# A hybrid block on one core: the token sums, first weights and weight sums of the seven products placed and ordered anew

## The chip, the cores and the metric

The kernel runs on one core of a Trainium2 chip. Its time is device microseconds of one execution. Five engines each work off a queue of their own in order: TensorE (PE: matmuls; PEld are its weight loads), VectorE (DVE), ScalarE (ACT), GpSimd (POOL) and SyncE (SP, which issues most transfers). They wait for each other by semaphores.

## The reference, cut to what matters

```python
def swiglu(x, w_gate, w_up, w_down):
    return (jax.nn.silu(x @ w_gate) * (x @ w_up)) @ w_down

def reference(x, ...):
    h = x                                             # 512 tokens x 1024
    f = swiglu(rms_norm(h, ffn1_norm_pre), ffn1_w_gate, ffn1_w_up, ffn1_w_down)   # hidden size 2816
    h = h + 0.5 * rms_norm(f, ffn1_norm_post)
    m = hybrid_mixer(rms_norm(h, mix_norm_pre), ...)  # attention and convolution, not touched here
    h = h + rms_norm(m, mix_norm_post)
    f = swiglu(rms_norm(h, ffn2_norm_pre), ffn2_w_gate, ffn2_w_up, ffn2_w_down)
    return h + 0.5 * rms_norm(f, ffn2_norm_post)
```

All is float32. Every operand of a matmul is kept as a high and a low part, and a product is three matmuls (high x high, high x low, low x high; `mm3`).

## The kernel before

**Stages.** The first feed-forward block (`ffn`), the mixer, the second `ffn`. The hidden dimension has 22 tiles of 128; each needs one block of gate weights and one of up weights, 128 x 1024 float32 of 512 KB. Weight blocks come in the order of use through three buffers (`raws`) by transfers on SyncE. `split` makes the two parts: ScalarE copies the high part, VectorE subtracts it and so gives the low part. The parts live in a ring of six pairs (`ring`, `whi` and `wlo`).

**Tiles 0 to 2** (`CLASSIC` = 3) are computed directly, each from a pair of blocks with 24 matmuls a block: "pair 0", "pair 1" and "pair 2" (the third pair) below. `hidden` ends a pair: a Silu on ScalarE, a multiplication on VectorE into `hid`. The first `ffn` opens with two pairs (its list of steps has four entries), on the first half of the tokens (`lo` = 0), then on the second half (`lo` = HALF), and computes pair 2 after them on all 512 tokens at once. The second `ffn` has six entries, so all three pairs are in that part. The tokens' own transposes (`turned0`, `turned2`) are steps in between.

**Tiles 3 to 21** go through seven products in place of eight, a scheme in Strassen's manner over two halves of the tokens and two of the inner dimension. `token_sums` makes, once, four sums s1 to s4 of the quadrants of u (`join` adds high and low part back together first; `early` joins the first half of the tokens, `first` the second half and makes s1, s2; `second` makes s4 and s3; `third` splits s3 into the place of quadrant (0, 1) of u). `weight_sums` makes for each tile four half blocks of weight sums: t13 (two subtractions on VectorE) and t24 (two on GpSimd, the second from the first). Each tile then has the operands b, t13, t24 (128 x 1024) and b22 (128 x 512), each split by `high` (ScalarE) and `low` (VectorE).

**A period.** A product is twelve matmuls with 256 columns. Period j (the loop in `seven_products`) runs the first three products of tile j (`first_products`: b x a11, t13 x s1, t24 x s2), the two last of tile j-1 (`third_products`), and two more of tile j (`second_products`: t13 x s3, then b x a12). Between them VectorE reads partial results out of a bank before the next product accumulates into it: the additions `add(xs[j][:, q[1]], ...)` and the like, line 346, tile xn. In the same period the operands of tile j+1 are made. The order is that of the code (`in_order`: TensorE, VectorE and ScalarE are not rescheduled there, GpSimd nowhere).

**After the run** `row_product` multiplies by the down weights; `act` splits rows of `hid`. Its weights are fetched and split by `prefetch`. The pools `ffn_gu` (sums, t13, t24, b22) and `ffn_d` (act) share memory one after the other.

**Norm weights.** `gpool` has two buffers of 128 x 1024 (name gain). `constants`, called in the middle of the first `ffn`, loads the gains of post and mix into them, on ScalarE's queue, with the mixer's constants and the table of relative positions (rel, tile xn, two small steps on VectorE, lines 563 and 564).

Of the kernel before, what the change touches and what calls it, by code (L numbers as in the profile page):

```python
# [8 lines left out]
F32 = mybir.dt.float32  # L9
# [43 lines left out]
def kernel(  # L53
# [238 lines left out]
    def token_sums(u, hid, gu):  # L292
# [8 lines left out]
        place3 = quadrant(u, 0, 1)  # L301
# [26 lines left out]
        return parts[0], parts[1], place3, parts[2], (early, first, second, third)  # L328

    def seven_products(u, sums, hid, gu, j0):  # L330
# [4 lines left out]
        s1, s2, s3, s4, (_, _, _, late) = sums  # L335
# [9 lines left out]
        def add(out, a, b, eng=nc.vector, op=ALU.add):  # L345
            eng.tensor_tensor(out=out, in0=a, in1=b, op=op)  # L346

        def weight_sums(j):

            gate, up = raw[j]  # L350
            t13 = gu.tile([P, 1024], F32, name="t13")
            t24 = gu.tile([P, 1024], F32, name="t24")
# [5 lines left out]
            ops[j] = {"b": (pair_tiles(), gate), "t13": (pair_tiles(), t13), "t24": (pair_tiles(), t24),  # L358
                      "b22": (b22, up[:, hi])}
# [34 lines left out]
        for n in ("b", "t13", "t24", "b22"):  # L394
            if n == "b":
                load(j0)
                weight_sums(j0)
            high(j0, n)
            low(j0, n)
        load(j0 + 1)  # L400
        for j in range(j0, NF + 1):
            p, n = j - 1, j + 1
            old, now, new = p >= j0, j < NF, n < NF
            if old:
                x, (g1, g2, g3) = xs[p], g[p]
                y = ys[p] = wide()
                add(x[:, q[2]], g2[:, q[0]], x[:, q[0]])
                add(y[:, q[3]], g3[:, q[0]], x[:, q[2]])
                silu(y[:, q[0]], g1[:, q[0]])
            if now:  # L410
                first_products(j)
            if new:
                weight_sums(n)
                high(n, "b")
                low(n, "b")
# [573 lines left out]
```

## Time and profile before

| | us |
|---|---|
| times of the runs shown | 1071.84, 1072.8, 1467.72 |
| their median | 1072.8 |
| the profiled execution | 1069.87 |
| its span | 1068.1 |
| TensorE busy in it | 1037.4 |

The profile is of one execution. A row of a timeline has start and length in us, engine, line, operation, tiles (written <- read), size, and, where the engine stood idle before, for how long and whom the instruction waited for. A matmul's row is longer than its share, since matmuls overlap in the pipe: read starts, not lengths. "First head" below is the stretch from the end of the classic pairs to the first full period in the first `ffn`, "second head" that in the second; "tail" is where the products end and the down weights begin.

### The profile page before, as it was taken

What the parts mean: (1) busy time and instruction counts of PE and PEld (TensorE: products, weight loads), DVE (VectorE), ACT (ScalarE), POOL (GpSimd) and SP (SyncE); (2) the same over time, 40 slices, a digit from 0 to 9 for tenths busy, and PEclk for the clock granted to TensorE, in tenths of its full rate; (3) what the DMA queues carried; (4) which work ended last, traced back from release to release, by engine and by line L of the source; (5) the groups of instructions that cost most, each with busy time, mean ns of one, the idle gap of its engine ahead of it and who ended that gap; (6) DMA issues with size and microseconds to landing.
All of it is one profiled execution on the core that took longest, in us unless ns stands there. A gap on an engine that the chain in (4) does not pass through costs nothing.

```text
span 1068.1 us, 16197 instructions
## 1 busy us (share of the span) xinstructions
PE 1037.4 (97%) x6527; PEld 942.2 (88%) x6527; DVE 801.9 (75%) x1112; ACT 479.2 (45%) x785; POOL 163.2 (15%) x118
## 2 busy tenths in 40 slices
PE   9869999999999999999999999998999999999997
PEld 8769999998888899888888888898999999978886
DVE  7589999997333477999969777479899999773324
ACT  6244444445222343477885354344444444352211
POOL 1043343340000010000000100012242442200000
PEclk9979999999999999999999999999899999999999
DMA  6133333334433133332321135131323333343301
GB/s 236 64 99 100 99 100 119 100 100 129 127 99 99 40 118 119 100 97 88 98 87 49 52 104 177 55 119 41 99 99 104 114 99 102 98 158 99 99 20 79
DMA packets 30046, 106.42 MB, mean 100 GB/s; under 512 B 3457, under 2 KB 4105, under 8 KB 29970
## 3 DMA queue, kind: packets, MB, share of 16 engines
q1 hardware_dynamic: 27648, 100.41, 29.5%
q10 hardware_dynamic: 2322, 4.97, 1.5%
q8 instruction: 51, 0.84, 0.3%
q14 instruction: 25, 0.20, 0.1%
HBM read 103.25 MB, written 2.12 MB: 99 GB/s over the span
## 4 chain that ended last, share of the span: by engine, by line
PE 88%; DVE 4%; issue 4%; DMA 2%; ACT 1%; POOL 1%; DVEq 0%; POOLq 0%; SPq 0%
PE ps L214 26%; PE ps L132 19%; PE ps L131 18%; PE ps L133 18%; PE ps L196 3%; DMA raw<-in_w 1%; DVE wlo L367 1%; PE ps L790 1%; PE ps L773 1%; POOL t L346 1%; PE ps L176 1%; PE ps L763 0%; PE ps L762 0%; DVE ul L93 0%; DMA h<-in_x 0%
## 5 line engine op out<-in xcount | busy, mean ns | idle before, releaser
L131 PE MATMUL ps<-uh,whi 128*128 128x256 f32 (+1 forms) x960 | 300.6, 313 | 15.7 <-DVE xn L346 11.7
L133 PE MATMUL ps<-uh,wlo 128*128 128x256 f32 (+1 forms) x960 | 298.1, 310 | 4.1 <-DVE wlo L367 4.1
L132 PE MATMUL ps<-ul,whi 128*128 128x256 f32 (+1 forms) x960 | 298.2, 311 | 1.0 <-DVE ul L93 1.0
L93 DVE TENSOR_TENSOR wlo<-raw,whi 128x1024 fp32r<-128x1024 f32 x108 | 131.5, 1220 | 134.5 <-ACT whi L92 134.4
L131 PEld LDWEIGHTS ps<-uh,whi 128*128 128x128 f32 x960 | 185.8, 194 | 24.8 <-ACT whi L363 14.4
L133 PEld LDWEIGHTS ps<-uh,wlo 128*128 128x128 f32 x960 | 185.6, 193 | 13.4 <-DVE wlo L367 4.4
L132 PEld LDWEIGHTS ps<-ul,whi 128*128 128x128 f32 x960 | 185.7, 193 | 9.5 <-DVE ul L93 1.6
L214 PE MATMUL ps<-whi,act 128*128 128x512 f32 x704 | 190.3, 390 | 1.8 <-ACT act L92 1.8
L92 ACT CAST whi<-raw 128x1024 fp32r<-128x1024 f32 x108 | 112.7, 1050 | 169.3 <-PE ps L214 131.9
L346 POOL TENSOR_TENSOR t<-raw,t 128x512 f32<-128x512 f32 x76 | 142.9, 1880 | 288.4 <-DVE t L346 285.4
L214 PEld LDWEIGHTS ps<-whi,act 128*128 128x128 f32 x704 | 131.9, 188 | 29.2 <-issue 2.2
L367 DVE TENSOR_TENSOR wlo<-t,whi 128x1024 fp32r<-128x1024 f32 x76 | 132.9, 1748 | 1.5 <-ACT whi L363 1.4
L363 ACT CAST whi<-t 128x1024 fp32r<-128x1024 f32 x76 | 79.7, 1049 | 116.3 <-PE ps L132 99.7
L214 PE MATMUL ps<-wlo,act 128*128 128x512 f32 x352 | 109.6, 389 | 0.0
L346 DVE TENSOR_TENSOR xn<-ps,xn 128x256 f32<-128x256 f32 x190 | 76.6, 416 | 17.3 <-PE ps L133 16.1
L367 DVE TENSOR_TENSOR wlo<-raw,whi 128x1024 fp32r<-128x1024 f32 x38 | 86.7, 2280 | 2.8 <-ACT whi L363 2.8
L601 DVE SCALAR_TENSOR_TENSOR acc<-c,ch,acc 128x512 f32<-128x512 f32 x120 | 86.1, 746 | 1.5
L214 PEld LDWEIGHTS ps<-wlo,act 128*128 128x128 f32 x352 | 66.1, 188 | 13.8
L159 POOL TENSOR_TENSOR rstd<-ms,mhalf 128x1 f32<-128x1 f32 x24 | 15.1, 628 | 388.9 <-DVE ms L155 388.5
L392 ACT ACTIVATE xn<-ps 128x256 f32<-128x256 f32 x38 | 14.6, 385 | 94.2 <-DVE xn L346 81.1
L346 DVE TENSOR_TENSOR t<-raw 128x512 f32<-128x512 f32 x76 | 48.8, 683 | 0.7 <-DVE b22l L367 0.6
L131 PE MATMUL ps<-s1h,whi 128*128 128x256 f32 x152 | 43.5, 286 | 0.0
(185 smaller groups left out, 1700.3 us busy)
## 6 DMA issues: line engine op xcount, KB each, us to landing
raw<-in_w SPq DMA_DIRECT2D x132, 512.0 KB, 3.5
raw<-in_wm SPq DMA_DIRECT2D x52, 512.0 KB, 3.6
gain<-in_gains ACTq DMA_DIRECT2D x5, 512.0 KB, 3.8
h<-in_x SPq DMA_DIRECT2D x4, 512.0 KB, 7.0
out<-h SPq DMA_DIRECT2D x3, 512.0 KB, 2.6
bias<-tab_d ACTq DMA_DIRECT2D x8, 128.0 KB, 3.1
bias<-tab_d ACTq DMA_DIRECT2D x8, 112.0 KB, 3.1
out<-xn SPq DMA_DIRECT2D x1, 256.0 KB
```

Of the source, the lines that this page charges most:

```text
L92: nc.scalar.copy(out=hi, in_=src)
L93: nc.vector.tensor_tensor(out=lo, in0=src, in1=hi.bitcast(F32), op=ALU.subtract)
L131: nc.tensor.matmul(ps, a[0], b[0], start=start, stop=False, **kw)
L132: nc.tensor.matmul(ps, a[0], b[1], start=False, stop=False, **kw)
L133: nc.tensor.matmul(ps, a[1], b[0], start=False, stop=stop, **kw)
L159: nc.gpsimd.tensor_tensor(r, ms, mhalf, op=ALU.pow)
L196: nc.tensor.matmul(ps[:, lo:hi], w[wi][:, k * P:(k + 1) * P], u[ui][:, k, lo:hi], start=i == 0 and k == 0, stop=i == 2 and k == KD - 1)
L214: nc.tensor.matmul(acc[n], a[ai], w[bi][:, n * 512:(n + 1) * 512], start=start and i == 0, stop=stop and i == 2)
L346: eng.tensor_tensor(out=out, in0=a, in1=b, op=op)
L363: nc.scalar.copy(out=h_, in_=src)
L367: nc.vector.tensor_tensor(out=l_, in0=src, in1=h_.bitcast(F32), op=ALU.subtract)
L601: nc.vector.scalar_tensor_tensor(acc[:, j, :], cs[j][:, w:w + S], wc, acc[:, j, :], op0=ALU.mult, op1=ALU.add)
```

## The change

- The joins of the first half of the tokens (`early`) become a step ahead of the last transposed tokens' split: in place of `step()` stands `(step or early)()`, and the lists have a None there.
- `third` goes: s3 is split in `second`, into the two buffers of `gpool`, not into u. The gains are loaded after the products (`late1`, `late2`).
- `weight_sums` becomes `sums13` and `sums24`, all four subtractions on VectorE; in a period t24's sums stand between b's and t13's parts.
- The preparation of tile 3 (`before`, a generator) is pulled forward: b, t13 and the t24 sums between pair 0's and pair 1's `hidden`, t24's parts ahead of `second`, b22 after pair 2's `hidden`. In the first `ffn` that is ahead of pair 2's products.
- In the last period the first two blocks of down weights and the first two rows of `hid` (`down_parts`, into a pair of the ring) are split while the products still run.

```diff
-        place3 = quadrant(u, 0, 1)
+        third = [gpool.tile([P, 4, HALF], F32R, name="gain") for _ in range(2)]
...
             nc.vector.tensor_tensor(out=s3, in0=whole[0, 0], in1=whole[0, 1], op=ALU.subtract)
-
-        def third():
-            split(*place3, s3)
+            split(*third, s3)
...
-        def weight_sums(j):
...
-            add(t24[:, lo], up[:, hi], t13[:, lo], nc.gpsimd, ALU.subtract)
-            add(t24[:, hi], gate[:, hi], t24[:, lo], nc.gpsimd, ALU.subtract)
+        def sums13(j):
...
+        def sums24(j):
+            gate, up = raw[j]
+            t24 = gu.tile([P, 1024], F32, name="t24")
+            add(t24[:, lo], up[:, hi], ops[j]["t13"][1][:, lo], op=ALU.subtract)
+            add(t24[:, hi], gate[:, hi], t24[:, lo], op=ALU.subtract)
...
+        def before():
+
+            load(j0)
+            sums13(j0)
+            parts(j0, "b")
+            parts(j0, "t13")
+            sums24(j0)
+            yield
+            parts(j0, "t24")
+            yield
+            parts(j0, "b22")
+            load(j0 + 1)
+
+        def down_parts(n):
+
+            for pair in pair_tiles()[0:n]:
+                a = pair[:, lo], pair[:, hi]
+                split(*a, hid[:, len(acts), :])
+                acts.append(a)
+
+        def periods():
...
+                if now:
+                    first_products(j)
+                if new:
+                    sums13(n)
+                    parts(n, "b")
+                elif now:
+                    prefetch(1)
+                if now:
+                    xs[j] = wide()
+                    nc.scalar.copy(out=xs[j][:, q[0]], in_=g[j][0][:, q[0]])
+                if new:
+                    sums24(n)
+                    parts(n, "t13")
+                elif now:
                     prefetch(2)
+                if now:
+                    add(xs[j][:, q[1]], g[j][1][:, q[0]], xs[j][:, q[0]])
+                if old:
+                    third_products(p)
+                    add(x[:, q[3]], g2[:, q[0]], x[:, q[0]])
+                if new:
+                    parts(n, "t24")
+                elif now:
+                    down_parts(2)
...
                         if lo == 0:
-                            early()
                             prefetch(2 * CLASSIC - head)
                             first()
+                    hidden(0, pss[0])
+                    next(before)
+                    hidden(1, pss[1])
                 if between:
                     with tc.issue_after(later["silu"].ins):
                         between()
                 with in_order():
-                    for j in range(head // 2, CLASSIC):
-                        ps = two_banks()
-                        for i in range(2):
-                            columns(weight(0), u, ps[i])
-                        hidden(j, ps)
+                    next(before)
                     second()
-                    seven_products(u, sums, hid, gu, CLASSIC)
-
+                    for j in range(2, CLASSIC):
+                        if j >= len(pss):
+                            pss.append(two_banks())
+                            for ps in pss[j]:
+                                columns(weight(0), u, ps)
+                        hidden(j, pss[j])
+                    next(before, None)
+                    periods()
+
+            late()
...
+    def late1():
+        later["post"] = gain(1)
+        later["mix"] = gain(2)
```

How the order moves at three places (names as in the program; the numbers tell buffers apart).

VectorE in the first head, up to the addition `xn<-ps` that reads tile 3's bank ahead of its second products; before, from the sum s3 (`hid<-hid`) on:

```order
L323 TENSOR_TENSOR hid_209<-hid_209 128x1024
L346 TENSOR_TENSOR t13_568<-raw_566,raw_564 128x512
L346 TENSOR_TENSOR t13_568<-raw_566 128x512
L367 TENSOR_TENSOR wlo_577<-raw_564,whi_576 128x1024
L367 TENSOR_TENSOR wlo_579<-t13_568,whi_578 128x1024
L367 TENSOR_TENSOR wlo_581<-t24_569,whi_580 128x1024
L367 TENSOR_TENSOR b22l_575<-raw_566,b22h_574 128x512
L346 TENSOR_TENSOR t13_633<-raw_592,raw_590 128x512
L346 TENSOR_TENSOR t13_633<-raw_592 128x512
L367 TENSOR_TENSOR wlo_642<-raw_590,whi_641 128x1024
L367 TENSOR_TENSOR wlo_644<-t13_633,whi_643 128x1024
L346 TENSOR_TENSOR xn_649<-ps_595,xn_649 128x256
```

and after the change, from s3 on (`gain` is the new place of the third sum's parts):

```order
L323 TENSOR_TENSOR hid_209<-hid_209 128x1024
L93 TENSOR_TENSOR gain_220<-hid_209,gain_219 128x1024
L474 TENSOR_TENSOR hid_209<-xn_585,ps_536 128x512
L372 TENSOR_TENSOR b22l_512<-raw_495,b22h_511 128x512
L344 TENSOR_TENSOR t13_633<-raw_592,raw_590 128x512
L344 TENSOR_TENSOR t13_633<-raw_592 128x512
L372 TENSOR_TENSOR wlo_637<-raw_590,whi_636 128x1024
L344 TENSOR_TENSOR t24_644<-raw_592,t13_633 128x512
L344 TENSOR_TENSOR t24_644<-raw_590,t24_644 128x512
L372 TENSOR_TENSOR wlo_639<-t13_633,whi_638 128x1024
L344 TENSOR_TENSOR xn_642<-ps_595,xn_642 128x256
```

The third sum's low part, pair 2's multiplication (L474) and two t24 subtractions have come ahead of the addition; the splits of tile 3's b, t13 and t24 have moved further up.

VectorE in the first head at pair 1's multiplication and the table of positions (`xn<-xn`); before:

```order
L453 TENSOR_TENSOR hid_209<-xn_491,ps_222 128x512
L563 TENSOR_SCALAR xn_500<-xn_500 8x257
L564 COPY xn_500<-xn_500 8x383
L453 TENSOR_TENSOR hid_209<-xn_557,ps_508 128x512
L321 TENSOR_TENSOR hid_209<-hid_209 128x1024
L93 TENSOR_TENSOR s4l_218<-hid_209,s4h_217 128x1024
```

and after the change:

```order
L344 TENSOR_TENSOR t24_508<-raw_495,t13_497 128x512
L344 TENSOR_TENSOR t24_508<-raw_493,t24_508 128x512
L474 TENSOR_TENSOR hid_209<-xn_515,ps_224 128x512
L586 TENSOR_SCALAR xn_520<-xn_520 8x257
L587 COPY xn_520<-xn_520 8x383
L372 TENSOR_TENSOR wlo_514<-t24_508,whi_513 128x1024
L321 TENSOR_TENSOR hid_209<-hid_209 128x1024
L93 TENSOR_TENSOR s4l_218<-hid_209,s4h_217 128x1024
```

The table's two steps stood ahead of pair 2's multiplication; now t24's low part and s4 follow them.

VectorE at the tail of the first run, before (`wlo<-raw` are down weights, `xn<-ps` the additions, `act` the first row of `hid`):

```order
L346 TENSOR_TENSOR xn_2731<-ps_2677,xn_2731 128x256
L346 TENSOR_TENSOR xn_2792<-ps_2678,xn_2731 128x256
L435 TENSOR_TENSOR hid_209<-xn_2792 128x512
L93 TENSOR_TENSOR wlo_2869<-raw_2866,whi_2868 128x1024
L93 TENSOR_TENSOR wlo_2875<-raw_2872,whi_2874 128x1024
L346 TENSOR_TENSOR xn_2835<-ps_2797,xn_2835 128x256
L93 TENSOR_TENSOR wlo_2950<-raw_2947,whi_2949 128x1024
L346 TENSOR_TENSOR xn_2902<-ps_2798,xn_2835 128x256
L346 TENSOR_TENSOR xn_2835<-ps_2797,xn_2835 128x256
L93 TENSOR_TENSOR wlo_2956<-raw_2953,whi_2955 128x1024
L346 TENSOR_TENSOR xn_2902<-ps_2798,xn_2835 128x256
L93 TENSOR_TENSOR act_2959<-hid_209,act_2959 128x512
```

and after the change:

```order
L93 TENSOR_TENSOR wlo_2836<-raw_2833,whi_2835 128x1024
L93 TENSOR_TENSOR wlo_2844<-raw_2841,whi_2843 128x1024
L344 TENSOR_TENSOR xn_2839<-ps_2795,xn_2839 128x256
L344 TENSOR_TENSOR xn_2722<-ps_2675,xn_2722 128x256
L93 TENSOR_TENSOR whi_2873<-hid_209,whi_2873 128x512
L93 TENSOR_TENSOR wlo_2874<-hid_209,wlo_2874 128x512
L344 TENSOR_TENSOR xn_2790<-ps_2676,xn_2722 128x256
L456 TENSOR_TENSOR hid_209<-xn_2790 128x512
L344 TENSOR_TENSOR xn_2839<-ps_2795,xn_2839 128x256
L344 TENSOR_TENSOR xn_2906<-ps_2796,xn_2839 128x256
L344 TENSOR_TENSOR xn_2839<-ps_2795,xn_2839 128x256
L344 TENSOR_TENSOR xn_2906<-ps_2796,xn_2839 128x256
```

The down weights and the first two rows of `hid` (`whi_2873`, `wlo_2874`) are split ahead of the last tile's additions.

## Rows read from the trace of the kernel before

**Rows 1.** The page: its busy time by engine, and a DMA issue.

```profile
PE 1037.4 (97%) x6527; PEld 942.2 (88%) x6527; DVE 801.9 (75%) x1112; ACT 479.2 (45%) x785; POOL 163.2 (15%) x118
...
gain<-in_gains ACTq DMA_DIRECT2D x5, 512.0 KB, 3.8
```

**Rows 2.** TensorE's waits: us in total, times, longest.

```profile
PE ps L131 <- DVE xn L346: 11.7, 4, 5.5
PE ps L133 <- DVE wlo L367: 4.1, 1, 4.1
PE ps L131 <- ACT whi L363: 4.0, 1, 4.0
PE ps L214 <- ACT act L92: 1.8, 2, 1.0
...
PE ps L132 <- DVE ul L93: 1.0, 2, 0.5
```

**Rows 3.** Timeline of TensorE, first head.

```profile
47.53 0.39 PE L133 MATMUL ps<-uh,wlo 128*128 128x512 f32 x1
...
67.64 0.55 PE L131 MATMUL ps<-uh,whi 128*128 128x256 f32 x1 [4.18 <-DVE xn L346]
...
73.16 0.28 PE L131 MATMUL ps<-uh,whi 128*128 128x256 f32 x1
```

**Rows 4.** Timeline of TensorE, second head.

```profile
749.52 0.55 PE L131 MATMUL ps<-uh,whi 128*128 128x256 f32 x1 [5.45 <-DVE xn L346]
...
755.39 0.28 PE L131 MATMUL ps<-uh,whi 128*128 128x256 f32 x1
```

**Rows 5.** Busy time of PE, PEld, DVE, ACT, POOL, then clock, DMA.

```profile
65.60:72.40 6.80, 4.27 (x18) 4.01 (x19) 5.69 (x8) 1.56 (x2) 0.48 (x1) 0.50 0.37 105
749.50:755.00 5.50, 4.99 (x22) 4.72 (x22) 4.39 (x7) 0.06 (x1) 0.07 (x1) 0.50 0.47 153
100.00:240.00 140.00, 140.00 (x1169) 140.00 (x1168) 138.07 (x167) 63.88 (x98) 52.94 (x28) 1.00 0.34 105
```

**Rows 6.** Timeline of TensorE, tail of the first run.

```profile
255.79 0.39 PE L131 MATMUL ps<-uh,whi 128*128 128x256 f32 x1 [1.04 <-DVE xn L346]
...
259.92 0.47 PE L214 MATMUL ps<-whi,act 128*128 128x512 f32 x1 [0.95 <-ACT act L92]
```

**Rows 7.** Timeline of VectorE and GpSimd, one period inside the first run.

```profile
93.09 0.88 DVE L346 TENSOR_TENSOR xn<-ps,xn 128x256 f32<-128x256 f32 x2
93.88 1.28 DVE L346 TENSOR_TENSOR t<-raw 128x512 f32<-128x512 f32 x2
95.08 2.32 DVE L367 TENSOR_TENSOR wlo<-raw,whi 128x1024 fp32r<-128x1024 f32 x1
97.32 2.31 DVE L367 TENSOR_TENSOR wlo<-t,whi 128x1024 fp32r<-128x1024 f32 x1
...
100.29 1.23 DVE L367 TENSOR_TENSOR wlo<-t,whi 128x1024 fp32r<-128x1024 f32 x1
...
103.16 0.88 DVE L346 TENSOR_TENSOR xn<-ps,xn 128x256 f32<-128x256 f32 x2
...
94.69 3.86 POOL L346 TENSOR_TENSOR t<-raw,t 128x512 f32<-128x512 f32 x2 [6.20 <-DVE t L346]
```

**Rows 8.** Timeline of VectorE, first head.

```profile
34.58 0.68 DVE L453 TENSOR_TENSOR hid<-xn,ps 128x512 f32<-128x512 f32 x1
...
39.33 0.28 DVE L563 TENSOR_SCALAR xn<-xn 8x257 f32<-8x257 f32 x1 [1.52 <-DMA xn<-in_rel]
...
50.96 1.23 DVE L93 TENSOR_TENSOR s4l<-hid,s4h 128x1024 fp32r<-128x1024 f32 x1 [1.11 <-ACT s4h L92]
```

**Rows 9.** Timeline of VectorE and ScalarE, second head.

```profile
719.83 1.29 DVE L93 TENSOR_TENSOR ul<-ps,uh 128x512 fp32r<-128x512 f32 x2 [2.63 <-ACT uh L92]
721.03 4.62 DVE L305 TENSOR_TENSOR hid<-uh,ul 128x1024 f32<-128x1024 f32 x4
...
729.27 1.28 ACT L452 ACT_TABLE_LOAD   x1
```

More of the change, by code (lines that the diff above doesn't have):

```diff
@@ L323, in second, with seven_products @@
             nc.vector.tensor_tensor(out=s3, in0=whole[0, 0], in1=whole[0, 1], op=ALU.subtract)
-        def third():
-            split(*place3, s3)
-        return parts[0], parts[1], place3, parts[2], (early, first, second, third)
-    def seven_products(u, sums, hid, gu, j0):
+            split(*third, s3)
+        return parts[0], parts[1], third, parts[2], (early, first, second)
+    def seven_products(u, sums, hid, gu, j0, acts):
         a11, a12, a22 = quadrant(u, 0, 0), quadrant(u, 1, 0), quadrant(u, 1, 1)
-        s1, s2, s3, s4, (_, _, _, late) = sums
+        s1, s2, s3, s4, _ = sums
         raw, ops, g, xs, ys = {}, {}, {}, {}, {}
@@ L392, in silu @@
             nc.scalar.activation(out=out, in_=src, func=AF.Silu)
[L394 to L415, printed above, removed]
-            if now:
-                xs[j] = wide()
-                nc.scalar.copy(out=xs[j][:, q[0]], in_=g[j][0][:, q[0]])
-            if new:
-                high(n, "t13")
-                low(n, "t13")
-            if now:
-                add(xs[j][:, q[1]], g[j][1][:, q[0]], xs[j][:, q[0]])
-            if j == j0:
-                late()
-            if old:
-                third_products(p)
-                add(x[:, q[3]], g2[:, q[0]], x[:, q[0]])
-            if new:
-                high(n, "t24")
-                low(n, "t24")
-            if old:
-                silu(y[:, q[1]], x[:, q[3]])
-                add(y[:, q[2]], g3[:, q[0]], x[:, q[1]])
-                nc.vector.tensor_tensor(out=hid[:, p, :], in0=y[:, lo], in1=y[:, hi], op=ALU.mult)
-            if new:
-                high(n, "b22")
-                low(n, "b22")
-            load(j + 2)
-            if now:
-                if n == NF:
-                    prefetch(2)
-                second_products(j)
@@ L445, in ffn @@
-    def ffn(u, steps, post, pre=None, turned=None, between=None, weave=False):
+        def before():
[14 more added lines that the diff above has]
+                acts.append(a)
@@ L447, in ffn @@
+        return before(), periods
+    def ffn(u, steps, post, late, pre=None, turned=None, between=None, weave=False):
         with tc.tile_pool(name="ffn_h", bufs=1) as hp:
@@ L455, in ffn @@
             with tc.tile_pool(name="ffn_gu", bufs=1) as gu:
+                acts = []
                 sums = token_sums(u, hid, gu)
-                early, first, second, _ = sums[-1]
+                early, first, second = sums[-1]
+                before, periods = seven_products(u, sums, hid, gu, CLASSIC, acts)
                 ws = []
@@ L555, in constants @@
     def constants():
-        later["post"] = gain(1)
-        later["mix"] = gain(2)
         nc.scalar.dma_start(out=ch, in_=chan)
@@ L893, with late2 @@
             row_product(KD, lambda k: part(m, ALLP, k), post_mix, pre2, turned2)
-    g_last = gain(5)
+    def late2():
+        later["last"] = gain(5)
     def post2(t, y):
         if t < NT - 1:
-            add_normed(t, y, g_last, 4.0)
+            add_normed(t, y, later["last"], 4.0)
             nc.sync.dma_start(out=out[t * P:(t + 1) * P, :], in_=h[:, t, :])
             return
-        tmp = wide()
+        tmp, g_last = wide(), later["last"]
         halves = [slice(0, D // 2), slice(D // 2, D)]
```

42 lines of the change are left out of this document (30 added, 12 removed).

## The prediction

> **What bounds the kernel now.** I read the page first, then TensorE's own waits, then its timeline around the two places where they lie, and last VectorE and GpSimd at those places. TensorE is busy for 1037.4 us of a span of 1068.1 [rows 1], so whatever this change gives back must come out of some 31 us. The list of TensorE's waits says where they are [rows 2]: 11.7 us in four waits for an addition on VectorE (xn, line 346), 4.1 for a low part of a weight, 4.0 for a high part, 1.8 for the first activations of the down product, 1.0 for low parts of u. All lie at the edges of the two runs of seven products; inside them nothing is named.
>
> The head of the first run: the last matmul of pair 2, the third, starts at 47.53; then tile 3 has five products ahead of the first full period, which starts at 73.16 [rows 3]. Undisturbed, a matmul comes every 0.12 us (1169 in 140 us [rows 5]), a product of twelve takes 1.44 and a period of seven 10.08, so that period could start at 47.65 + 5 x 1.44 = 54.9: 18.3 us are lost. In the second run the three first products are done at 744.07 without a wait, then TensorE stands for 5.45 us, goes on at 749.52 and begins the full period at 755.39 [rows 4]; it could have begun 2 x 1.44 after the three, at 746.8, so 8.6 are lost. Part of each loss is the clock: after an idle stretch of 4.18 us the granted clock was 0.50, the 1.2 GHz level, from 65.6 to 72.4, and after the 5.45 us again, while the long stretch inside the run is at 1.00, 2.4 GHz [rows 5]. At the tail of a run there are two waits of about 1 us [rows 6]; with the second run's alike (the 11.7 less 4.18, 5.45 and this 1.04 leaves 1.04; the 1.8 holds both others [rows 2]) that makes 3.9. All together 18.3 + 8.6 + 3.9 = 30.8 us, the most that can be had.
>
> **The sums on VectorE.** Inside the runs TensorE is busy for all of 140 us and VectorE for 138.1 of them [rows 5]: two engines at the limit, and the change gives VectorE two more subtractions in each period. What they cost depends on the rows of one period [rows 7]. VectorE's row from one pair of additions to the next, 93.09 to 103.16, is 10.07 us long. In it two splits of a whole block take 2.32 and 2.31 us, a third of the same size 1.23. GpSimd's two subtractions run from 94.69 to 98.55, just beside the two long ones; the short one has GpSimd idle. I read that the first two are held up by GpSimd, by 2 x 1.09 us, and that this goes with it. The two sums as VectorE's own pair costs 1.28 [rows 7], and 0.1 more, as the second half needs the first. Net -2.2 + 1.4 = -0.8: about 9.3 us of work in a period that TensorE makes 10.08 long. So the body of the run neither gains nor loses; all 36 periods that prepare a next tile stay at 10.08. Cover for the added 1.4 us is this slack; without it each period would pay what is over.
>
> The Trainium skill, Perfetto Trace Analysis, section "Optimizing Scalar/DVE Operations", says that a saturated VectorE may be relieved by handing work to ScalarE or even GpSimd, and so speaks against taking it back; it adds that handing over between VectorE and GpSimd might not help, since they share a read port. By its first half alone the time would be that of the slow rival below; the rows here (2.3 us beside GpSimd, 1.23 without) are on the side of the second.
>
> **The first head (18.3 us lost).** After the change everything waits in VectorE's one queue. TensorE's next obstacle is the same as before: the first product of the third sum accumulates into the bank that the addition xn (line 346, now 344) has to read first, and that addition now stands behind the whole preparation of tile 3, the third sum and most of tile 4's. From the multiplication that ends pair 0 (34.58 before [rows 8], the same now, as the sums ahead of it are only reordered) the order lists: three such multiplications (0.68 each), the two pairs of t13 sums (1.28 each), the two pairs of t24 sums (1.4 each), s4 and s3 (1.23 each, as s4l [rows 8]), s4l and third low (1.23 each), b low, t13 low and t24 low of tile 3 and b low and t13 low of tile 4 (1.23 each, [rows 7]), b22 low (0.68), the two table steps (0.28 [rows 8] and about as much), the addition (0.44). Sum: 2.04 + 2.56 + 2.8 + 4.92 + 6.15 + 0.68 + 0.6 + 0.44 = 20.2 us. Independent neighbours start some 0.08 us before the one ahead has ended (95.08 + 2.32 against 97.32 [rows 7]): 16 times, -1.3.
>
> To that come waits inside the queue. s4l waits for ScalarE's cast, 1.11 us [rows 8], as before; third low does so in the same way now, 1.11 more. The table's first step waits for the transfer of rel, 1.52 us before [rows 8]. Now that wait stands ahead of t24 low, s4, s3 and all of tile 4, and TensorE waits for these; bounds are 0 (the gains no longer go ahead of it in its queue) and 1.5, and I take 0.7. So the addition ends at 34.58 + 20.2 - 1.3 + 2.2 + 0.7 = 56.4. TensorE, which ends pair 2 at about 47.9 and the first three products at 52.2, stands for 4.3 us and starts its second products at about 56.5, against 67.64 [rows 3].
>
> Both idle stretches of that length in [rows 3, 4] were followed by the slow clock [rows 5], so I let the two products take what they took in the second run, 749.52 to 755.39, less the 0.5 for low parts of u in it [rows 2, 4], which goes as those parts now come earlier: 5.4 us. The full period starts at 61.9 in place of 73.16: **-11.3**. With the clock kept, the two take 2.9 and it is -13.8; with 1.5 for the table it is -10.5. What could be late next are the raw blocks of tile 4: the second takes the buffer of tile 3's gate, which is now free once the t24 sums are done, by the list above near 40 us, and which is not needed before 51.
>
> Two edits at this head I cost at about nothing. The joins of the first token half, set ahead of the last split of u, push that split back by their own 2.35 us (half of 4.62 [rows 9]); 24 matmuls of 0.12 stand before TensorE needs it, so 0 to 2.3, and 0.3 taken, already in the 47.9. One matmul of the third pair slips ahead among those of pair 0: the same work, elsewhere. The gains' loads, gone from ScalarE's queue here, were beside other work.
>
> **The second head (8.6 us lost).** Here pair 2 belongs to the first half, and there is little to win. The first joins fit into the 2.63 us in which VectorE waited ahead of the last split [rows 9], so the other two end near 723.4, not 725.65. s1, s2 and their two low parts take 4 x 1.23 to 728.3; the first Silu, behind its table load of 1.28 [rows 9], lets pair 0's multiplication start at about 728.9. From there the same queue of 20.2 - 1.3, without the table steps (-0.6), with the two waits of 1.11 and about 0.5 for the cast of t24: 728.9 + 21.0 = 749.9. TensorE goes on at about 750.0, where it was 749.52. What the joins and the missing GpSimd give (2.3 and about 4 x 1.1) is taken back by the two pairs of t24 sums (2.8), the third sum's low part ahead of the addition (1.2) and waits for casts that filled no gap before (2.7). The 0.5 inside the second products goes: **0**, with 1 us either way.
>
> **The tails.** In the last period the additions of line 344 no longer stand behind low parts of down weights, and act 0 and 1 are split there from buffers of the ring that are already free, so both waits should go: **-3.9**; 0 if the transfers of these weights come late, since each raw buffer comes free only with the last tile's splits. The post gain's load now waits on ScalarE until the third sum's last reader is done; behind it stands only the last Silu, which needs a later product anyway. It lands in 3.8 us [rows 1], and the first row of the down product ends some 100 us later: 0.
>
> **Sum.** -11.3 + 0 - 3.9 = -15.2 against the profiled execution's own 1069.87: 1054.7. Of the runs shown the two that agree are 1071.84 and 1072.8, in the middle 1072.3 and 2.4 above that execution, so for a timed run I forecast 1054.7 + 2.4: **1057 us**, 1.5% below 1072.8.
>
> **Rivals.** *The whole wait goes*, as the change's words would have it, with every part ready when TensorE comes: 1072.3 - 30.8 = 1041. Against it stands the addition behind 20 us of queue; it would need VectorE's queue to be some 4 us shorter at one head and 6 at the other. 0.05. *The slow one*: VectorE becomes the bound of each period. If the two long splits stay at 2.3 us without GpSimd (because of other traffic, or because they are long by their place), a period needs 10.07 + 1.4 less VectorE's idle 0.14; at 11.3 against 10.08, 36 periods cost 44 us, and with the heads and tails paid back the time is near 1072 + 44 - 15 = 1101. It decides from the point where VectorE's period passes 10.08. For it: 138.1 busy of 140; against it: the 1.23 us split between them. 0.04. The first half of the Trainium skill's rule above leads here too. *Less comes back*: the tails keep their waits (3.9), and the first head loses 1 to 3 us more, to the table or to a raw block that comes late: 1072.3 - 11.3 + 1 to 3, so 1062 to 1064. For it: the more is packed ahead, the more hangs on one late transfer. Against it: the buffers come free earlier than before. 0.14. The forecast, with either clock: 0.77.
>
> **Range and chances.** The bounds of the forecast are 1072.3 less 10.5 - 1 + 0 and less 13.8 + 1 + 3.9, so 1062.8 and 1053.6; going beyond them on the low side for waits that I have added up too strictly and on the high side for the third rival's better half gives 1049 to 1064. Over 2% faster means below 1051.3, about the least that a measurement of this kernel tells from no change: the first rival and the low edge, 0.09. Slower by over 2%: 0.04. The rest, 0.87, is within 2%.
>
> **What would show it.** Right, step by step: no GpSimd work inside the runs, and block splits of 1.2 us throughout; TensorE at 10.08 us a period with VectorE near 90% busy; in the first head one TensorE wait of some 4 us, for the addition at line 344, ending near 56.5; in the second head the same wait, some 6 us; no wait at either tail. Wrong: splits of 2.3 us without GpSimd, periods above 10.1, a first wait at another instruction (third's low part, or a raw block), or no half clock after the wait.

## The result and the profile after

The changed kernel takes 1052.8 us (median of 1051.82 to 1054.05) beside 1072.3 for the kernel before on the same chip: a ratio of 0.9823 [0.9803, 0.9842]. The forecast was 1057, with a range of 1049 to 1064. The profiled execution took 1053.61, with a span of 1051.6, 16.5 less than before.

The page's line of busy time by engine (answers to [rows 1]):

```profile
PE 1033.8 (98%) x6527; PEld 939.2 (89%) x6527; DVE 775.4 (74%) x1188; ACT 479.9 (46%) x785; POOL 20.8 (2%) x42
```

TensorE's waits (us in total, times, longest; answers to [rows 2]):

```profile
PE ps L131 <- ACT b22h L368: 9.8, 2, 6.3
PE ps L275 <- POOL ident masks.py:199: 1.3, 1, 1.3
```

GpSimd is out of the runs. Of the waits at the heads two are left, both at the first product of the third sum; the tails [rows 6] have none. TensorE's timeline at the two heads (start, length, row, idle before; answers to [rows 3, 4]):

```profile
57.83 0.55 PE L131 MATMUL ps<-gain,whi 128*128 128x256 f32 x1 [3.50 <-ACT b22h L368]
...
62.04 0.28 PE L131 MATMUL ps<-uh,whi 128*128 128x256 f32 x1
...
737.08 0.55 PE L131 MATMUL ps<-gain,whi 128*128 128x256 f32 x1 [6.33 <-ACT b22h L368]
...
741.29 0.28 PE L131 MATMUL ps<-uh,whi 128*128 128x256 f32 x1
```

The full periods start at 62.04 (73.16 before) and 741.29 (755.39). VectorE's timeline in the first head, and its addition in the second (answers to [rows 8, 9]):

```profile
36.40 0.68 DVE L474 TENSOR_TENSOR hid<-xn,ps 128x512 f32<-128x512 f32 x1
...
42.55 0.28 DVE L586 TENSOR_SCALAR xn<-xn 8x257 f32<-8x257 f32 x1
...
46.64 1.23 DVE L93 TENSOR_TENSOR s4l<-hid,s4h 128x1024 fp32r<-128x1024 f32 x1 [1.12 <-ACT s4h L92]
...
50.12 1.23 DVE L93 TENSOR_TENSOR gain<-hid,gain 128x1024 fp32r<-128x1024 f32 x1 [1.12 <-ACT gain L92]
...
57.26 0.42 DVE L344 TENSOR_TENSOR xn<-ps,xn 128x256 f32<-128x256 f32 x1
...
736.51 0.42 DVE L344 TENSOR_TENSOR xn<-ps,xn 128x256 f32<-128x256 f32 x1
```

TensorE goes on 0.15 us after each addition has ended (57.68 and 736.93), although the waits name ScalarE's cast of b22, which ends a little later still (57.80 and 737.06). Which of the two it is, an experiment has to say: the addition first, below. The table's step at 42.55 has no wait in front of it any more. VectorE in one period (answers to [rows 7]):

```profile
92.79 1.28 DVE L344 TENSOR_TENSOR t<-raw 128x512 f32<-128x512 f32 x2
93.98 1.22 DVE L372 TENSOR_TENSOR wlo<-raw,whi 128x1024 fp32r<-128x1024 f32 x1
95.12 1.42 DVE L344 TENSOR_TENSOR t<-raw,t 128x512 f32<-128x512 f32 x2
96.45 1.22 DVE L372 TENSOR_TENSOR wlo<-t,whi 128x1024 fp32r<-128x1024 f32 x1
...
102.87 1.28 DVE L344 TENSOR_TENSOR t<-raw 128x512 f32<-128x512 f32 x2
```

All splits of a block take 1.22 now. Windows behind the two waits and inside the run (start and end, length, busy PE, PEld, DVE, ACT and POOL with their instructions, then the granted clock; answers to [rows 5]):

```profile
57.83:60.70 2.87, 2.87 (x13) 2.87 (x14) 1.58 (x2) 0.00 (x0) 0.00 (x0) 0.50 0.60 184
60.75:62.00 1.25, 1.25 (x12) 1.25 (x12) 1.20 (x3) 0.00 (x0) 0.00 (x0) 1.00 0.77 292
737.08:739.90 2.82, 2.82 (x13) 2.82 (x14) 1.58 (x2) 0.00 (x0) 0.00 (x0) 0.50 0.59 183
100.00:240.00 140.00, 140.00 (x1169) 140.00 (x1169) 125.14 (x193) 63.77 (x98) 0.00 (x0) 1.00 0.35 107
```

### The profile page after: what moved, and what is told of

Its sections match the earlier page's. It is cut to its first block, busy times and chain, and to the rows that moved or that the text cites. A ratio compares the mean times of both kernels' runs of the same rounds, so it can differ in the third digit from the quotient of the medians.

```text
span 1051.6 us, 16123 instructions
## 1 busy us (share of the span) xinstructions
PE 1033.8 (98%) x6527; PEld 939.2 (89%) x6527; DVE 775.4 (74%) x1188; ACT 479.9 (46%) x785; POOL 20.8 (2%) x42
## 4 chain that ended last, share of the span: by engine, by line
PE 90%; DVE 6%; ACT 2%; issue 1%; POOL 0%; DVEq 0%; POOLq 0%; ACTq 0%
PE ps L214 27%; PE ps L131 19%; PE ps L133 19%; PE ps L132 19%; PE ps L196 3%; DVE t L344 1%; PE ps L817 1%; DVE wlo L372 1%; PE ps L176 1%; PE ps L800 1%; DVE hid L305 1%; DVE acc L628 1%; DVE wlo L93 0%; ACT whi L368 0%; PE ps L279 0%
## 5 line engine op out<-in xcount | busy, mean ns | idle before, releaser
L131 PE MATMUL ps<-uh,whi 128*128 128x256 f32 (+1 forms) x808 | 254.6, 315 | 0.0
L133 PE MATMUL ps<-uh,wlo 128*128 128x256 f32 (+1 forms) x808 | 252.8, 313 | 0.0
L132 PE MATMUL ps<-ul,whi 128*128 128x256 f32 (+1 forms) x808 | 252.6, 313 | 0.0
L93 DVE TENSOR_TENSOR wlo<-raw,whi 128x1024 fp32r<-128x1024 f32 x108 | 131.8, 1222 | 135.7 <-ACT whi L92 134.3
L133 PEld LDWEIGHTS ps<-uh,wlo 128*128 128x128 f32 x808 | 154.1, 191 | 9.0
L132 PEld LDWEIGHTS ps<-ul,whi 128*128 128x128 f32 x808 | 154.4, 191 | 8.2 <-DVE ul L93 0.2
L131 PEld LDWEIGHTS ps<-uh,whi 128*128 128x128 f32 x808 | 154.4, 191 | 7.9
L368 ACT CAST whi<-t 128x1024 fp32r<-128x1024 f32 x76 | 79.7, 1049 | 110.6 <-PE ps L132 94.8
L372 DVE TENSOR_TENSOR wlo<-t,whi 128x1024 fp32r<-128x1024 f32 x76 | 92.9, 1223 | 18.8 <-ACT whi L368 18.7
L131 PE MATMUL ps<-gain,whi 128*128 128x256 f32 x152 | 44.3, 292 | 9.8 <-ACT b22h L368 9.8
L344 DVE TENSOR_TENSOR t<-raw,t 128x512 f32<-128x512 f32 x76 | 52.4, 689 | 1.3
L372 DVE TENSOR_TENSOR wlo<-raw,whi 128x1024 fp32r<-128x1024 f32 x38 | 46.4, 1220 | 1.6 <-ACT whi L368 1.5
L132 PE MATMUL ps<-gain,whi 128*128 128x256 f32 x152 | 44.1, 290 | 0.0
```

The costliest lines, as they stand in the source:

```text
L93: nc.vector.tensor_tensor(out=lo, in0=src, in1=hi.bitcast(F32), op=ALU.subtract)
L131: nc.tensor.matmul(ps, a[0], b[0], start=start, stop=False, **kw)
L132: nc.tensor.matmul(ps, a[0], b[1], start=False, stop=False, **kw)
L133: nc.tensor.matmul(ps, a[1], b[0], start=False, stop=stop, **kw)
L344: nc.vector.tensor_tensor(out=out, in0=a, in1=b, op=op)
L368: nc.scalar.copy(out=h_, in_=src)
```

## The experiments

Differences are against 1052.8; the kernel before ran beside each group at 1071.4 to 1072.2. Waits come from each run's own profile, which is one execution; its span can differ from the median by what the start does (see "The rest" below).

**The sums back on GpSimd.**

```diff
-            add(t24[:, lo], up[:, hi], ops[j]["t13"][1][:, lo], op=ALU.subtract)
-            add(t24[:, hi], gate[:, hi], t24[:, lo], op=ALU.subtract)
+            nc.gpsimd.tensor_tensor(out=t24[:, lo], in0=up[:, hi], in1=ops[j]["t13"][1][:, lo], op=ALU.subtract)
+            nc.gpsimd.tensor_tensor(out=t24[:, hi], in0=gate[:, hi], in1=t24[:, lo], op=ALU.subtract)
```

> The changed kernel with one part undone: the two t24 subtractions of each tile go back to GpSimd; everything else stays. My theory: the sums' place costs and gives nothing in the body. The two long splits of a period go back from 1.22 to about 2.3 us, the period stays 10.08 and TensorE busy throughout. At the heads VectorE loses two subtractions (1.4 us) per tile and two splits beside GpSimd grow by 1.1 each, for two tiles: +1.7 us, so the addition that TensorE waits for ends 1 to 2 us later at each head: some 3 us in all, about 1056 against 1052.8. Rival A: the sums on VectorE are what gives the gain, in the body; then the period here is above 10.08 or a wait stands in each, 36 periods of at least 0.3 us, 1064 or more. Rival B: the sums on VectorE cost the heads their 1.4 us a tile and the long splits hide; then the heads are 2.8 us shorter each and the time is about 1047.

1055.8, ratio 0.9854 [0.9840, 0.9868]. VectorE's timeline of one period:

```profile
94.35 2.33 DVE L372 TENSOR_TENSOR wlo<-raw,whi 128x1024 fp32r<-128x1024 f32 x1
96.61 2.31 DVE L372 TENSOR_TENSOR wlo<-t,whi 128x1024 fp32r<-128x1024 f32 x1
...
99.57 1.23 DVE L372 TENSOR_TENSOR wlo<-t,whi 128x1024 fp32r<-128x1024 f32 x1
```

The window inside the run, columns as above:

```profile
100.00:240.00 140.00, 140.00 (x1169) 140.00 (x1168) 135.63 (x166) 63.89 (x98) 49.34 (x26) 1.00 0.35 108
```

The long splits are back and VectorE is busier with less to do, 135.6 against 125.1; TensorE is busy throughout all the same. The waits at the heads are 4.50 and 7.35, 1.0 longer each; that is 2.0 of the 3.0 us, and the half clock behind them, which lasts longer in this profile, can give the rest. So GpSimd's work beside a split costs VectorE 1.1 us a split, and it shows only where VectorE's queue is waited for.

**The sums on VectorE in the kernel before, alone**: `nc.gpsimd` becomes `nc.vector` in both lines of `weight_sums`.

> The kernel before with one part of the change alone: the two t24 subtractions of a tile on VectorE in place of GpSimd, in the old order. My theory: the body does not change (10.08 us a period); the heads win what GpSimd cost them, two long splits of a tile at 1.1 us each less 1.4 for the subtractions, and the wait for GpSimd's own 3.9 us: 2 to 5 us in all, 1067 to 1070 against 1072.2. Rival A: the sums' place is the whole gain: 1056 or less. Rival B: VectorE becomes the bound of the period: 1080 or more.

1069.3, ratio 0.9977 [0.9968, 0.9986], a gain of 2.8 us by the medians: the same part from the other side. The profiled execution was one of the slowest of its runs (1071.65 of 1067.21 to 1071.99), so its span says nothing of the gain; its waits for the addition are shorter than before (11.7 in [rows 2]):

```profile
PE ps L131 <- DVE xn L346: 9.0, 4, 4.9
```

**The addition first.**

```diff
                     nc.scalar.copy(out=xs[j][:, q[0]], in_=g[j][0][:, q[0]])
+                    if j == j0:
+                        add(xs[j][:, q[1]], g[j][1][:, q[0]], xs[j][:, q[0]])
...
-                if now:
+                if now and j > j0:
                     add(xs[j][:, q[1]], g[j][1][:, q[0]], xs[j][:, q[0]])
```

> The changed kernel with one row moved, in the first period of each run only: the addition that reads the three first products' bank goes ahead of tile 4's t24 sums and t13 low part in VectorE's queue. My theory: TensorE waits at the heads (3.50 us from 54.33, 6.33 us from 730.75) for this addition behind VectorE's queue, though the trace names ScalarE's cast of b22. The three operations that it passes take 2.5 us, so both waits become 2.5 us shorter: 1.0 and 3.8, that is 5 us; where the clock is kept after the short wait, 1.7 us more (3.4 us at half clock): 1046 to 1048. Rival A: the cast that the trace names is the releaser: both waits stay, 1052.8. Rival B: tile 4's t13 and t24 low parts are late instead, so the wait moves to its first products: 1051 to 1053.

1047.8, ratio 0.9777 [0.9762, 0.9793]. TensorE's waits:

```profile
PE ps L131 <- DVE xn L344: 4.6, 2, 3.8
```

The waits are 0.83 and 3.80, shorter by 2.7 and 2.5, and the profile now names the addition. No half clock follows the short one (the granted clock is 1.00 from 53.20 to 56.00). At the first head TensorE goes on at 53.20, and ScalarE's cast of b22 starts only at 55.46. So the addition is the releaser; the cast, named before, had only ended at the same time.

**Both moved**: in addition s3 goes ahead of s4's split.

```diff
+            nc.vector.tensor_tensor(out=s3, in0=whole[0, 0], in1=whole[0, 1], op=ALU.subtract)
             split(*parts[2], s4)
-            nc.vector.tensor_tensor(out=s3, in0=whole[0, 0], in1=whole[0, 1], op=ALU.subtract)
             split(*third, s3)
```

> The changed kernel with two rows moved: as in the run with the addition first, and the subtraction s3 put ahead of s4's split, so that neither split waits 1.12 us for its cast. My theory: the waits at the heads are VectorE's queue and nothing else. That queue gets 2.2 us shorter, so the second head's wait goes from 3.80 to about 1.6 and the first head's stays near 0.8 (there the three products' end is the limit), and the clock stays at its upper level at both: 2.2 us and up to 1.7 for the clock under the run with the addition first (1047.8), 1044 to 1045.5. Rival: the casts are late by other work on ScalarE, or what is late next is tile 4's own low parts: 1047 to 1048.

1042.1, ratio 0.9728 [0.9715, 0.9740], 10.7 below the changed kernel and better than expected. TensorE's waits:

```profile
PE ps L131 <- DVE xn L344: 2.0, 2, 1.5
```

VectorE's timeline, the addition at each head:

```profile
52.32 0.42 DVE L344 TENSOR_TENSOR xn<-ps,xn 128x256 f32<-128x256 f32 x1 [0.68 <-PE ps L133]
...
725.78 0.42 DVE L344 TENSOR_TENSOR xn<-ps,xn 128x256 f32<-128x256 f32 x1
```

Two windows, with the clock third from the end:

```profile
50.00:60.00 10.00, 9.41 (x79) 9.21 (x78) 9.12 (x13) 5.06 (x7) 0.00 (x0) 1.00 0.53 159
720.00:735.00 15.00, 13.54 (x113) 13.34 (x113) 14.90 (x21) 8.63 (x12) 0.00 (x0) 1.00 0.35 106
```

At the first head VectorE itself waits for TensorE now. Behind waits of 0.59 and 1.46 the clock stays at its upper level. The waits sum to 2.05 in place of 9.83 (7.8 us). In the profiles the two heads are 9.8 us shorter, so the clock gives some 2.0; the remaining 0.9 of the 10.7 is not assigned.

**The queue in the old order** at the heads: pair 2 and its multiplication, then `second`, then tile 3's preparation.

```diff
                     hidden(0, pss[0])
-                    next(before)
                     hidden(1, pss[1])
...
-                    next(before)
-                    second()
                     for j in range(2, CLASSIC):
...
                         hidden(j, pss[j])
-                    next(before, None)
+                    second()
+                    for _ in range(3):
+                        next(before, None)
```

> The changed kernel with the old order of the queue at the head: pair 2's products and its multiplication first, then s4 and the third sum, then tile 3's preparation; the sums on VectorE, the third sum's place, the joins and the tails stay as changed. My theory: this order is the large term. At the first head VectorE has nothing to do until pair 2 ends near 50, then 20 us of queue to the addition, so TensorE's second products start near 70 and the full period near 75 in place of 62.0; at the second head pair 2 is done early and nothing changes: 12 to 14 us in all, 1065 to 1067 against 1052.8. Rival: the gain of the first head comes from what is in the queue (no GpSimd, third sum's place, table without wait) and not from its order: 1057 or less.

1078.9, ratio 1.0068 [1.0055, 1.0082]: 26 us lost, twice what was expected. TensorE's waits:

```profile
PE ps L131 <- ACT whi L368: 15.0, 2, 7.5
PE ps L131 <- DVE xn L344: 10.1, 2, 5.1
PE ps L133 <- DVE wlo L372: 3.9, 3, 1.9
```

VectorE's timeline, the multiplication for pair 2 at each head:

```profile
48.13 0.69 DVE L474 TENSOR_TENSOR hid<-xn,ps 128x512 f32<-128x512 f32 x1 [9.41 <-PE ps L133]
...
738.09 0.69 DVE L474 TENSOR_TENSOR hid<-xn,ps 128x512 f32<-128x512 f32 x1 [5.07 <-PE ps L133]
```

The first head loses 13.7 us (TensorE goes on at 69.53, 11.7 later than in the changed kernel, in an execution that was 2.0 ahead before the head), as expected. That is also 1.9 behind the 67.64 of the kernel before [rows 3]: what the change puts into the queue gains nothing at this head; its order does. That the second would lose nothing was wrong: VectorE stands 5.07 us for pair 2 there too, with all the preparation behind it, and that head loses another 12. The kernel before had that multiplication behind tile 3's splits at its second head, so there this order isn't the old one.

**The joins at their old place**, `early()` behind the last split of u.

> The changed kernel with the two joins of the first token half back at their old place, behind the last split of u. My theory: at the first head TensorE's products set VectorE's start in that stretch and the joins move nothing (0 to 2 us earlier for the last split, not waited for); at the second head the joins no longer fill VectorE's wait ahead of that split, so everything behind is 2.3 us later and the second wait goes from 6.33 to 8.6: 1055 against 1052.8. Rival: the early joins delay the last split of u and with it TensorE or the queue; then undoing them gives time back: 1051 or less.

1057.6, ratio 0.9871 [0.9858, 0.9884]. The second wait is 8.59, as expected, the first 3.76, so the waits are 2.5 us longer together. The span is 3.4 longer, the rest being half clock behind them; the median is 4.7 longer, and the 1.3 between is not explained.

**The third sum in u, split ahead of pair 2**: `third = quadrant(u, 0, 1)`.

> The changed kernel with the third sum's two parts in the quadrant of u, as before, but split at the changed place (ahead of pair 2's end), and the norm weights' buffers left free. My theory: its high part now must wait for pair 2's last use of that quadrant, some 49.5 us at the first head where ScalarE makes it at 49.03 now, so VectorE's queue behind it is 0.5 to 1.5 us later there, and at the second head, where pair 2 ends earlier against the queue, nothing: 1053 to 1054.5. The third sum's place is then worth about nothing. Rival: the place is what lets the split go ahead, and without it the queue stalls for the most of pair 2: the first wait grows by 4 us or more and the time is 1057 or above.

1065.7, ratio 0.9952 [0.9939, 0.9965], and no test of the question. In the program the split now stands ahead of pair 2's products, so in the first run these read the third sum where u's quadrant was: the kernel computes something else, and TensorE waits for the split:

```profile
PE ps L131 <- ACT uh L92: 10.9, 1, 10.9
```

**The third sum in u, split behind pair 2's products**; the engines' orders are those of the changed kernel.

> The changed kernel with the third sum's two parts in the quadrant of u again, split behind pair 2's products in the program; VectorE's and ScalarE's orders are as in the changed kernel, only the buffers differ. My theory: the high part waits for pair 2's last use of the quadrant, which comes within 1 us of the time at which ScalarE makes it now (cast at 49.03, pair 2's end near 49.7 in the profile after), so the queue and the addition behind it move by 0.5 to 1.5 us at the first head and by nothing at the second: 1053 to 1054.5 against 1052.8, and the norm weights' place is worth next to nothing. Rival: the place is what lets the third sum be split ahead of TensorE's need; without it the first wait grows by 4 us or more: 1057 or above.

1054.7, ratio 0.9837 [0.9824, 0.9851]. The waits are 3.36 and 6.40, as in the changed kernel (3.50 and 6.33), so the third sum's place is worth nothing at the heads. In this profile the first head is 1.2 us longer and the second 0.9, both by a longer half clock; behind the first wait it lasts to 62.8 in place of 60.7. The run with the old tails, below, whose heads are unchanged, is 1.3 and 0.9 longer at them in the same way, so I don't put the 1.9 us down to the sum's place. The window behind the first wait:

```profile
56.86:62.80 5.94, 5.94 (x28) 5.94 (x29) 3.64 (x6) 0.44 (x2) 0.00 (x0) 0.50 0.51 163
```

**The tails as before**: no `prefetch` and `down_parts` in the last period, `prefetch(2)` ahead of its `second_products`.

> The changed kernel with the last period as it was before: the down product's first weights and first two activations are prepared behind the run and not in the last period's gaps. My theory: the two waits of about 1 us at each tail come back, 3.9 us in all, at the places where they stood, nothing else moves: about 1056.7 against 1052.8. Rival: the tails have become short by other parts of the change (no GpSimd there, no splits beside it); then nothing changes, 1052.8.

1066.2, ratio 0.9946 [0.9928, 0.9965]: 13.4 us, where 3.9 were expected. TensorE's waits:

```profile
PE ps L214 <- ACT act L92: 3.7, 2, 2.3
PE ps L131 <- DVE xn L344: 2.1, 2, 1.0
```

ScalarE's timeline at the second tail:

```profile
926.50 0.34 ACTq L137 DMA_DIRECT2D gain<-in_gains  x1
```

The chain there (start, length, what):

```profile
927.57 5.04 DMA raw<-in_w
...
932.63 1.05 ACT whi L92
```

The old tail's waits are there, but those for the first row of `hid` are 1.33 and 2.33 us long where they were 0.95 and 0.85. At the second tail the third down weight lands 5.04 us after its buffer came free, and the first row of `hid` is cast behind it. One microsecond ahead of it the norm weights' load was issued. In this profile the tails cost 6.8 us, the clock at the first head 1.3, the mixer and the second head 1.1; it was the shortest of its runs (up to 1067.9).

**The old tails with the norm weights loaded early**, and the third sum in u, split behind pair 2's products.

> The run with the third sum in u (1054.7) and the old tails, with the norm weights loaded at their old, early places too. The question is why the old tails alone cost 13 us and not 3.9. My theory: there the norm weights' load is issued at 926.50 on ScalarE and shares the transfer time with the third weight of the down product (5.04 us from buffer to landing, 3.47 in the kernel before), so the first part of the down product waits 1.3 and 2.3 us in place of 0.9, and more weights come late behind it. With the loads early the tails cost what they cost before: waits of 1.04 and some 0.9 at each, 3.9 us in all: 1058 to 1060. Rival: the late load is harmless and the old tails are worse for another reason: 1064 or above again.

1058.9, ratio 0.9887 [0.9870, 0.9905], 4.2 over the run with the third sum in u and the new tails (1054.7). TensorE's waits:

```profile
PE ps L131 <- DVE xn L346: 2.1, 2, 1.0
PE ps L214 <- ACT act L92: 1.6, 2, 0.8
```

The same transfer in its chain:

```profile
923.96 3.45 DMA raw<-in_w
```

It takes 3.45 us in place of 5.04, and the waits are 3.6 in all: with the loads early the old tails cost what they cost before. The run differs from the old tails alone in the third sum's place too, and the old tails with the sum in u and the loads late were not run. That the late load is the cause is argued from the transfer's rows, and the sum's place is not excluded. In the profiles the difference is some 2 us (the tails cost 4.7 here, 6.8 above); the rest of the 13.4 in the longer runs was not profiled and stays open.

**More work for VectorE**: the second t24 subtraction of a tile made once, then twice more, behind the first two tiles.

```diff
             add(t24[:, hi], gate[:, hi], t24[:, lo], op=ALU.subtract)
+            if j > j0 + 1:
+                add(t24[:, hi], gate[:, hi], t24[:, lo], op=ALU.subtract)
```

> The changed kernel with one of the t24 subtractions made twice (the same values written again) for each tile behind the first two of a run, so the heads are as they were and each of some 34 periods gives VectorE 0.66 us more. My theory: VectorE has 9.0 us of work in a period that TensorE makes 10.08 long (125.1 busy of 140), so the period stays 10.08 with 9.7 of work, and the time stays: 1052 to 1054 against 1052.8. Rival: the waits for TensorE and ScalarE that stand in VectorE's period (0.23 and 0.53 in the profile) can't be filled, so there is no slack of this size, and the period grows by 0.3 or more: 1062 or above.

> The same with two such subtractions more, 1.3 us in each of some 34 periods. My theory: 9.0 + 1.3 = 10.3 us of work passes the 10.08 of the period, so VectorE becomes its bound: 10.3 to 10.9 with waits that stay, 34 x 0.25 to 0.8, so 1061 to 1080. This is the slow rival of the prediction made real, and the distance to it is the cover of the sums. Rival: TensorE remains the bound, since operations overlap: 1052 to 1055.

1053.8, ratio 0.9835 [0.9821, 0.9848], and 1070.7, ratio 0.9987 [0.9978, 0.9997]. The window inside the run, with one more:

```profile
100.00:240.00 140.00, 140.00 (x1169) 140.00 (x1168) 132.81 (x206) 64.17 (x98) 0.00 (x0) 1.00 0.33 107
```

The same window with two more:

```profile
100.00:240.00 140.00, 136.86 (x1115) 134.23 (x1115) 136.74 (x214) 62.01 (x94) 0.00 (x0) 1.00 0.30 99
```

TensorE's waits with two more:

```profile
PE ps L131 <- DVE xn L344: 7.7, 32, 0.3
```

VectorE's additions one period apart, with two more:

```profile
98.31 0.75 DVE L344 TENSOR_TENSOR xn<-ps,xn 128x256 f32<-128x256 f32 x2
...
108.88 0.75 DVE L344 TENSOR_TENSOR xn<-ps,xn 128x256 f32<-128x256 f32 x2
```

With one more VectorE has 9.6 us of work in a period (132.81 of 140, times 10.08) and nothing moves; the span is 1051.6 as in the changed kernel. With two more TensorE waits for the addition in nearly every period and makes 1115 matmuls where it made 1169: a period takes 10.57 us (98.31 to 108.88).

## Why the prediction held, term by term

The steps of the prediction are the ones that the runs show, but the number is hit by its margin: 1052.8 lies within 1049 to 1064 and just below 1053.6, the lowest sum of the prediction's own terms.

**The first head** (forecast -11.3): -13.0. The full period starts 11.1 earlier, in an execution whose beginning was 1.9 later (below). From pair 0's multiplication to the addition's end the forecast said 21.8, the profile has 57.68 - 36.40 = 21.3: the 0.7 for the table's wait didn't come. The step now starts 3.64 us behind the issue of its transfer (38.91 to 42.55); before, its wait ended 3.72 behind the issue (35.61 to 39.33). So the step's later place in the queue alone would have left under 0.1 of the wait, even with the gains' loads ahead of the transfer. The clock came back earlier than assumed [rows 5]: the two products took 4.2 in place of 5.4. That is luck: behind the same wait of 3.50 us, in the run with the old tails, the half clock lasted twice as long, and what follows the wait took 1.3 us longer. The window behind that wait there:

```profile
57.60:63.60 6.00, 6.00 (x28) 6.00 (x29) 3.64 (x6) 0.50 (x2) 0.00 (x0) 0.50 0.48 165
```

The run with the old queue shows that the order of the queue is what gives this term: 13.7 the other way.

**The second head** (0, either way 1): -0.8. The wait grew from 5.45 to 6.33, as forecast, the 0.5 inside the products is gone, and they too took 4.2. So the -0.8 is again the clock's early return. That the rest stays near nothing is a balance: the early joins give 2.3 of the wait, the sums' move off GpSimd 1.0 net of their own time, and the two waits for casts, which s3 moved ahead of s4's split removes, take back 2.3. The third sum's low part, 1.2 by the forecast's list, was not undone by itself.

**The body** (0): 0. 125.1 of 140 are 9.0 us of a period, forecast 9.3. The runs with more work put the slow rival's point between 9.6 and 10.3 us. The Trainium skill, Perfetto Trace Analysis, section "Optimizing Scalar/DVE Operations", says that a saturated VectorE may hand work over even to GpSimd. The run with the sums back on GpSimd speaks against that here: 3 us slower, with VectorE busier. Its second half, that the two share a read port, agrees with 2.33 against 1.22; no run shows that the port is the reason.

**The tails** (-3.9): -4.9, from TensorE's matmuls on either side of the two tails (-2.5 and -2.4). The forecast took the waits' own lengths, and these are too small as a price. At the first tail of the kernel before the matmuls start at 254.47 and 255.79, 1.32 apart where 0.12 is the rule: 1.20 lost, and the row says 1.04, because it counts from the end of the matmul ahead, whose row is 0.28 long. The first matmul behind the wait then takes 0.23 to the next start in place of 0.12. Some 0.25 for each of four waits is the missing 1.0. Undone alone the tails cost more than they gave, as the term for the gains' late loads, put at 0, holds only with the new tails: there the first two down weights are split before the loads are issued (921.37 at the second tail). I had costed the two edits apart.

**The rest.** +1.9 at the start and +0.3 in the mixer complete -16.5. The start is TensorE's first matmuls: the same pair in TensorE's timeline, in the kernel before:

```profile
4.25 1.12 PE L279 MATMUL ps<-xn,ones 1*128 1x512 f32 x2
```

and in the changed one:

```profile
4.31 2.07 PE L279 MATMUL ps<-xn,ones 1*128 1x512 f32 x2
```

Nothing was changed there, and of the twelve profiles of the changed kernel and its variants eight have a short pair (1.12 to 1.43) and four the long one. The granted clock reads 1.00 in both windows (4.30 to 7.40), so the rows don't say why. That the runs of the kernel before lie near 1070.3 or near 1072.3 fits with it; but two variants with the long pair (old tails, late joins) were profiled in the fastest of their runs, so it is not the only thing that varies. The profile therefore understates the gain. The medians' -19.5 is 4.3 more than the forecast's -15.2: 1.7 in the first head, 0.8 in the second and 1.0 at the tails, less 0.3 in the mixer, and some 1 that the profiles don't assign.

**The rival "the whole wait goes"** (1041, chance 0.05) was refuted for this change, for the reason given: the addition behind 20 us of queue. Two moved rows bring it to 1042.1.

**The parts don't add up.** Undone one at a time, the queue's order, the tails, the joins, the sums' place and the third sum's place cost 26.1, 13.4, 4.7, 3.0 and 1.9 us: 49 in all, where the whole change gains 19.5. Each was undone with the others in place, so none of these numbers is that part's share of the gain.

## What to carry to other kernels

When an engine stands idle at the edge of a steady loop, add up the in-order queue of the engine that it waits for: the gain was in the order of that queue, and what the waiting instruction needs belongs ahead of what only later work needs. An engine with slack inside the loop can still be the bound at its edges, where here 1 us of queue cost 1 us, and the clock's fall besides. Cost edits whose transfers meet in time together: the late load cost nothing that shows beside the new tails, and with the old ones it met a weight that TensorE was waiting for.

## What the runs showed of the hardware

The half clock behind a wait did not scale with the wait. Behind waits of 0.59, 0.83, 1.46 and 2.33 us (the last at the second old tail) the granted clock stayed at 1.00; but behind one of 2.05 and, a matmul later, one of 0.57, in the kernel before with the sums on VectorE, it was 0.50 (68.97 to 73.00). So the length of the wait alone does not tell. Behind 3.50 it was 0.50 for 2.9 us in the changed kernel and for 6.0 with the old tails, behind 3.36 (third sum in u) for 5.9. And the first matmuls of a program took 1.12 to 1.43 or 2.07 us a pair in different profiles with nothing changed there: about 2 us of the time. Each kernel has one profile, so no run shows directly that this pair is what splits the times of one kernel.
